# Order of the gathered tiles' work in an expert-lookup layer: dot products of both tiles ahead of the sums of both

## The chip, the cores and the metric

The kernel runs on one core of a Trainium2 chip. The metric is the device time of one execution in microseconds (us). A program of this kind keeps five engines and sixteen DMA engines busy side by side: TensorE (PE in the profile, with its weight loads as PEld), VectorE (DVE), ScalarE (ACT), GpSimd (POOL, which issues the indirect gathers here) and SyncE (SP, which issues the plain loads).

## The reference

Two transformer blocks run one after the other over 512 tokens of width 1024. The change touches only the last layer of the second block. For each token that layer picks 8 x 16 = 128 of 16,384 experts, takes the dot product of the token with each picked row of `peer_u`, applies gelu and a gate, and adds up the picked rows of `peer_v` with these factors:

```python
def chunk(args):
    hc, ec, gc = args
    u = peer_u[ec]
    a = jax.nn.gelu(jnp.einsum("ckd,cd->ck", u, hc).astype(jnp.float32)) * gc
    vv = peer_v[ec]
    return jnp.einsum("ck,ckd->cd", a.astype(vv.dtype), vv)
```

The result is added to the residual and normalised once more.

## The kernel before, in words

The 512 tokens are four tiles of 128. The kernel treats them in two ways at once, inside `peer`:

- **Dense tiles (2 and 3).** All 16,384 experts are computed. `u_tile(n)` (L1721) loads 512 KB of `peer_uT` by SP and makes 128 experts x 256 tokens on TensorE (L1726), with the gelu on ScalarE (L1728). `gates` (L1731) builds 0/1 masks on VectorE (L1759, L1760, L1764), multiplies them on TensorE (L1748, a *product*) and scales the stored activations on VectorE (L1752, *big*). `v_tile(n)` (L1772) loads 512 KB of `peer_v` and adds its four matmuls (L1776) into four accumulators.
- **Gathered tiles (0 and 1).** Only the picked rows are fetched. `row` (L1795) is one indirect DMA on the POOL queue: 128 rows of 4 KB, 512 KB, into one of 12 shared buffers (`rtile`, L1792). `dots` (L1801) fetches one row set of `peer_u` per slot and lets VectorE take its dot product (L1804), 128 slots for a tile. `factors` (L1808) makes the factors of a tile. `v_sum` (L1818) takes four row sets of `peer_v` and adds them up with eight TensorE matmuls (L1825), 32 sums for a tile. `last_norm` (L1832) finishes a tile.

The dense work is a fixed list `seq` of 256 tiles: 94 u tiles, then v and u tiles in turn until the 128th u tile, then the other v tiles. After each tile `fill` (L1864) takes gathered work from the generator `gather_units` (L1843), 1.4 row sets for each of the first 50 tiles and 2.3 after each later one. So the generator's order is the order in which gathered work enters all engines' queues, and each queue is worked off in its order. In the kernel before, the generator yields all dots of tile 0, then one sum of tile 0 and four dots of tile 1 in turn, then the sums of tile 1:

```python
yield from dots(0, 0, 128)
factors(0)
...
        if t == 0:
            yield from dots(1, 4 * r, 4 * r + 4)
```

The gate work is made in three batches of 32 steps: beside u tiles 50 to 93 (16 experts wide), beside the first 16 pairs of v and u tiles (64 wide), and beside v tiles 34 to 79 (48 wide). A row buffer is given out in turn: a gather waits until the work on the row set that lay there twelve gathers earlier is over, which is a dot on VectorE or a sum on TensorE.

Of the kernel before, what the change touches and what calls it, by code (L numbers as in the profile page):

```python
# [31 lines left out]
class Kern:  # L32
# [1430 lines left out]
    def peer(self):  # L1463
# [3 lines left out]
        GT, DT, DW = (0, 1), (2, 3), 256  # L1467
# [4 lines left out]
        with ExitStack() as ctx:  # L1472
# [5 lines left out]
            def pu(shape=(128, 512)):  # L1478
                return pp.tile(list(shape), F32, tag="u", name=self.nm("pu"), bufs=2)
# [4 lines left out]
            def pr(shape=(128, 512)):  # L1484
                return pp.tile(list(shape), F32, tag="r", name=self.nm("pr"), bufs=2)
# [309 lines left out]
            def row(src, idx):  # L1795
                u = rtile("u")
                nc.gpsimd.indirect_dma_start(out=u[:], out_offset=None, in_=A[src],  # L1797
                                             in_offset=bass.IndirectOffsetOnAxis(ap=idx, axis=0))
                return u

            def dots(t, s0, s1):  # L1801
                for s in range(s0, s1):
                    u = row("peer_u_2", ei[t][:, s:s + 1])
                    nc.vector.tensor_tensor_reduce(u[:], u[:], h3[t][:], scale=1.0, scalar=0.0, op0=OP.mult, op1=OP.add,  # L1804
                                                   accum_out=ga_t[t][:, s:s + 1])
                    yield 1

            def factors(t):  # L1808
                act(ga_t[t][:], ga_t[t][:], AF.Gelu_apprx_tanh)
                tt(ga_t[t][:], ga_t[t][:], gg[t][:], op=OP.mult)  # L1810
                p = pu([128, 4, 128])
                nc.tensor.transpose(p[:, 0, :], ga_t[t][:], self.ident[:])
                act(aT[t][:].rearrange("p g r -> p (g r)"), p[:, 0, :], AF.Copy)

            def v_rows(t, r):
                return [row("peer_v_2", eT[t][:, 32 * g + r:32 * g + r + 1]) for g in range(4)]

            def v_sum(t, r, us, acc):  # L1818

                w = wz[r % 4]  # L1820
                act(w[:, :, 31], aT[t][:, :, r], AF.Copy)  # L1821
                with ExitStack() as order:

                    for i, (c, g) in enumerate(itertools.product(range(2), (3, 0, 1, 2))):
                        m = nc.tensor.matmul(acc[c][32 * g:32 * g + 32, :], w[:, g, 31 - r:63 - r],  # L1825
                                             us[g][:, c * 512:c * 512 + 512], start=r == 0, stop=r == 31, skip_group_check=True)
                        if i == 0:
                            order.enter_context(tc.issue_after(m.ins))
# [3 lines left out]
            def last_norm(t, acc):  # L1832
                gf, x, o = rtile("gf"), rtile("xe"), rtile("xo")
                nc.gpsimd.dma_start(gf[:], rows(A["normf_g_2"], D))
                nc.gpsimd.dma_start(x[:], self.x3d[t * 128:t * 128 + 128, :])
                for c, cs in enumerate(hv):
                    tt(x[:, cs], x[:, cs], acc[c][:], op=OP.add)
                r = self.rstd([x[:, cs] for cs in hv], [o[:, cs] for cs in hv])
                for cs in hv:
                    stt(o[:, cs], x[:, cs], r[:], gf[:, cs], op0=OP.mult, op1=OP.mult)  # L1840
                    nc.sync.dma_start(self.out[t * 128:t * 128 + 128, cs], o[:, cs])

            def gather_units():  # L1843

                yield from dots(0, 0, 128)
                factors(0)
                for t in GT:
                    acc = [pr(), pr()]
                    us = v_rows(t, 0)
                    yield 4  # L1850
                    for r in range(32):
                        nx = v_rows(t, r + 1) if r < 31 else None
                        v_sum(t, r, us, acc)
                        yield 4 if r < 31 else 0
                        us = nx
                        if t == 0:
                            yield from dots(1, 4 * r, 4 * r + 4)
                    if t == 0:
                        factors(1)
                    last_norm(t, acc)  # L1860

            units = gather_units()

            def fill(n):  # L1864
# [141 lines left out]
```

## Time and profile before

| what | value |
|---|---|
| runs shown | 2919.39, 2919.87, 2923.93 us (median 2919.87) |
| the profiled execution's own time | 2930.82 us |
| its span | 2929.1 us |
| mean granted TensorE clock | 0.972 |
| PE busy in the span | 2717.2 us (93%) |
| DVE busy | 1848.5 us (63%) |
| POOL busy | 723.5 us (25%) |
| moved by DMA | 752.10 MB, mean 257 GB/s |

The layer in question begins at about 1742 us of the span, with the first u tile. The busy share of an engine over the whole span says little here. What counts is, stretch by stretch of this layer, which engine is never kept waiting, and what ends the waits of the others.

### The profile page before, as it was taken

What the parts mean: (1) busy time and instruction counts of PE and PEld (TensorE: products, weight loads), DVE (VectorE), ACT (ScalarE), POOL (GpSimd) and SP (SyncE); (2) the same over time, 40 slices, a digit from 0 to 9 for tenths busy, and PEclk for the clock granted to TensorE, in tenths of its full rate; (3) what the DMA queues carried; (4) which work ended last, traced back from release to release, by engine and by line L of the source; (5) the groups of instructions that cost most, each with busy time, mean ns of one, the idle gap of its engine ahead of it and who ended that gap; (6) DMA issues with size and microseconds to landing.
All of it is one profiled execution on the core that took longest, in us unless ns stands there. A gap on an engine that the chain in (4) does not pass through costs nothing.

```text
span 2929.1 us, 38343 instructions
## 1 busy us (share of the span) xinstructions
PE 2717.2 (93%) x13730; PEld 1907.3 (65%) x13730; DVE 1848.5 (63%) x3907; ACT 1019.7 (35%) x1672; POOL 723.5 (25%) x679
## 2 busy tenths in 40 slices
PE   7999969999999879999999889989989898699998
PEld 4776757777777667766678778877745554244333
DVE  5562569998888858998535399968557522452001
ACT  5442348777777653445633332200100000000000
POOL 1000050000000110101000343566543444444440
PEclk9999979999999989999999999999999999899999
DMA  7226568989999842322222348899988899999995
GB/s 258 87 86 215 206 212 324 355 319 354 351 351 348 317 148 86 108 72 66 89 91 94 119 166 284 335 409 409 360 326 318 327 362 350 324 355 360 369 375 184
DMA packets 228689, 752.10 MB, mean 257 GB/s; under 512 B 28160, under 2 KB 28448, under 8 KB 228496
## 3 DMA queue, kind: packets, MB, share of 16 engines
q1 hardware_dynamic: 145936, 458.69, 43.7%
q0 software_dynamic: 81984, 289.89, 27.1%
q8 instruction: 109, 1.79, 0.3%
q10 hardware_dynamic: 576, 1.05, 0.1%
q14 instruction: 84, 0.69, 0.1%
HBM read 736.90 MB, written 16.81 MB: 257 GB/s over the span
## 4 chain that ended last, share of the span: by engine, by line
PE 40%; DVE 9%; DMA 7%; issue 6%; POOL 2%; ACT 1%; DVEq 0%; another core or an unknown queue 0%; POOLq 0%; SPq 0%; ACTq 0%
PE pw L1776 12%; DMA u<-in_peer_u_dram,ei 6%; PE pu L1726 4%; PE pm L136 4%; PE pm L138 4%; PE pm L137 4%; PE pr L1825 3%; POOL u L1797 2%; DVE u L1804 2%; PE pa L1305 2%; DVE cv L1236 1%; PE pu L1748 1%; PE po L1334 1%; PE pw L138 1%; PE pw L136 1%
## 5 line engine op out<-in xcount | busy, mean ns | idle before, releaser
L84 DVE TENSOR_TENSOR lo<-raw,hi 128x1024 fp32r<-128x1024 f32 (+1 forms) x580 | 624.4, 1107 | 234.3 <-ACT hi L83 214.0
L83 ACT ACTIVATE hi<-raw 128x1024 fp32r<-128x1024 f32 (+1 forms) x600 | 556.9, 952 | 445.1 <-PE pm L137 197.0
L1804 DVE CUSTOM_DVE_ANT_0 u<-u,h 128x1024 f32<-128x1024 f32 x256 | 311.3, 1226 | 305.3 <-DMA u<-in_peer_u_dram,ei 258.7
L1726 PE MATMUL pu<-hd,raw 128*128 128x256 f32 x2048 | 474.1, 390 | 17.4 <-issue 8.3
L1776 PE MATMUL pw<-raw,big 128*128 128x512 f32 x1024 | 471.4, 609 | 6.7 <-DVE big L1752 6.7
L1726 PEld LDWEIGHTS pu<-hd,raw 128*128 128x128 f32 x2048 | 394.3, 195 | 94.9 <-issue 30.2
L1776 PEld LDWEIGHTS pw<-raw,big 128*128 128x128 f32 x1024 | 191.2, 193 | 252.7 <-issue 244.0
L1797 POOL DMA_INDIRECT u<-in_peer_v_dram,eT x256 | 259.2, 1012 | 378.5 <-DVE ga L1804 210.1
L1797 POOL DMA_INDIRECT u<-in_peer_u_dram,ei x256 | 288.4, 1126 | 204.7 <-issue 54.3
L1728 ACT ACTIVATE big<-pu 128x256 f32<-128x256 f32 x128 | 48.9, 384 | 492.6 <-PE pu L1726 430.8
L137 PE MATMUL pm<-lo,xth 128*128 128x512 f32 x512 | 204.8, 400 | 6.5 <-DVE lo L84 6.5
L136 PE MATMUL pm<-hi,xth 128*128 128x512 f32 x512 | 202.1, 395 | 0.0
L138 PE MATMUL pm<-hi,xtl 128*128 128x512 f32 x512 | 201.3, 393 | 0.0
L1236 DVE SCALAR_TENSOR_TENSOR cv<-z,cols,cv 128x496 f32<-128x496 f32 (+27 forms) x240 | 167.2, 735 | 0.5
L905 POOL DMA_INDIRECT yd<-y,idx x16 | 27.6, 1726 | 540.1 <-DVE y L1009 536.6
L138 PE MATMUL pm<-hT,lo 128*128 128x512 f32 x384 | 151.2, 395 | 0.0
L136 PE MATMUL pm<-hT,hi 128*128 128x512 f32 x384 | 151.1, 394 | 0.0
L137 PE MATMUL pm<-hT,hi 128*128 128x512 f32 x384 | 151.0, 393 | 0.0
L1821 ACT ACTIVATE wz<-aT 128x4 f32<-128x4 f32 x64 | 12.8, 209 | 396.9 <-PE pr L1825 396.8
L1825 PE MATMUL pr<-u,wz 128*32 128x512 f32 x1024 | 126.4, 612 | 8.3 <-DMA u<-in_peer_v_dram,eT 8.3
L137 PEld LDWEIGHTS pm<-lo,xth 128*128 128x128 f32 x512 | 96.4, 188 | 40.3 <-DVE lo L84 19.7
L1748 PEld LDWEIGHTS <-o 128*128 128x128 f16 x1536 | 55.0, 98 | 87.5 <-DVE big L1752 43.2
(575 smaller groups left out, 4323.8 us busy)
## 6 DMA issues: line engine op xcount, KB each, us to landing
raw<-in_w_gate_dram SPq DMA_DIRECT2D x128, 512.0 KB
raw<-in_w_up_dram SPq DMA_DIRECT2D x128, 512.0 KB
raw<-in_w_down_dram SPq DMA_DIRECT2D x128, 512.0 KB
raw<-in_peer_uT_dram SPq DMA_DIRECT2D x128, 512.0 KB
raw<-in_peer_v_dram SPq DMA_DIRECT2D x128, 512.0 KB
raw<-in_w_in_dram SPq DMA_DIRECT2D x104, 256.0 KB
wa<-in_w_ada_dram SPq DMA_DIRECT2D x48, 512.0 KB
raw<-in_w_in_dram SPq DMA_DIRECT2D x28, 512.0 KB
```

The lines of the kernel that those rows point to most:

```text
L83: return (self.nc.scalar.activation(hi, src, AF.Copy), (eng or self.nc.vector).tensor_tensor(lo, src, hi.bitcast(F32), op=OP.subtract))
L84: (eng or self.nc.vector).tensor_tensor(lo, src, hi.bitcast(F32), op=OP.subtract))
L136: mm(ps, a[0], b[0], start=first, stop=False, **kw)
L137: mm(ps, a[0], b[1], start=False, stop=False, **kw)
L138: return mm(ps, a[1], b[0], start=False, stop=last, **kw)
L1236: stt(a[:, d:], z[:, :512 - d], self.col("conv_w", k * 31 + j), a[:, d:], op0=OP.mult, op1=OP.add)
L1726: self.u_last = nc.tensor.matmul(p[:, :DW], raw[:, k, :], hd[k // 4][:, k % 4, :], start=k == 0, stop=k == KD - 1)
L1748: nc.tensor.matmul(p[:, i, :], o2[:, i // 2, :, i % 2], og[j][:, i // 2, :, i % 2], start=j == 0, stop=j == 1)
L1776: self.pace = nc.tensor.matmul(acc[t][c][:], a[:, t * 128:t * 128 + 128], raw[:, c * 512:c * 512 + 512], start=n == 0, stop=n == 127)
L1797: nc.gpsimd.indirect_dma_start(out=u[:], out_offset=None, in_=A[src], in_offset=bass.IndirectOffsetOnAxis(ap=idx, axis=0))
L1804: nc.vector.tensor_tensor_reduce(u[:], u[:], h3[t][:], scale=1.0, scalar=0.0, op0=OP.mult, op1=OP.add, accum_out=ga_t[t][:, s:s + 1])
L1825: m = nc.tensor.matmul(acc[c][32 * g:32 * g + 32, :], w[:, g, 31 - r:63 - r], us[g][:, c * 512:c * 512 + 512], start=r == 0, stop=r == 31, ...
```

## The change

The generator first yields all dots of tile 0 and tile 1, each followed by its factors, and then the sums of tile 0 and tile 1. Nothing is added or left out; the pace of `fill` stays as it is.

```diff
 def gather_units():
 
-    yield from dots(0, 0, 128)
-    factors(0)
+    for t in GT:
+        yield from dots(t, 0, 128)
+        factors(t)
     for t in GT:
         acc = [pr(), pr()]
         us = v_rows(t, 0)
...
             v_sum(t, r, us, acc)
             yield 4 if r < 31 else 0
             us = nx
-            if t == 0:
-                yield from dots(1, 4 * r, 4 * r + 4)
-        if t == 0:
-            factors(1)
         last_norm(t, acc)
```

What this does to the queues shows at two places. The first is the POOL queue in the middle of the former alternation, some fifty gathers after the last one of tile 0's dots (`in_peer_u_dram` is a row set for a dot, `in_peer_v_dram` one for a sum). Before:

```order
L1797 DMA u_18950<-in_peer_u_dram,ei_14586 128x1024
L1797 DMA u_18953<-in_peer_v_dram,eT_14587 128x1024
L1797 DMA u_18955<-in_peer_v_dram,eT_14587 128x1024
L1797 DMA u_18957<-in_peer_v_dram,eT_14587 128x1024
L1797 DMA u_18959<-in_peer_v_dram,eT_14587 128x1024
L1797 DMA u_19042<-in_peer_u_dram,ei_14586 128x1024
L1797 DMA u_19078<-in_peer_u_dram,ei_14586 128x1024
```

The same place of the queue in the changed kernel:

```order
L1797 DMA u_18922<-in_peer_u_dram,ei_14586 128x1024
L1797 DMA u_18925<-in_peer_u_dram,ei_14586 128x1024
L1797 DMA u_18961<-in_peer_u_dram,ei_14586 128x1024
L1797 DMA u_18964<-in_peer_u_dram,ei_14586 128x1024
L1797 DMA u_19006<-in_peer_u_dram,ei_14586 128x1024
```

The row sets for sums have moved behind the last dot of tile 1; four and four in turn have become one kind only.

The second is VectorE's queue in the second gate batch (`eq`, `o`, `og` are the masks, `big` the scaled activations, `ISA u_...,ga` a dot). Before:

```order
L1804 ISA u_19624,ga_15834<-u_19624,h_14592 128x1024
L1804 ISA ga_15834 128x1
L1752 SCALAR_TENSOR_TENSOR big<-pu_19394,big 128x34x8
L1752 SCALAR_TENSOR_TENSOR big_17146<-pu_19394,big_17146 128x30x8
L1759 TENSOR_TENSOR o_4214_19452<-io,e2b 128x1024
L1764 TENSOR_TENSOR og_19456<-eq_19453,gp_14595 128x512
L1764 TENSOR_TENSOR og_19458<-eq_19453,gp_14596 128x512
L1760 TENSOR_TENSOR eq_19509<-io,e1b 128x512
L1764 TENSOR_TENSOR og_19512<-eq_19509,gp_14595 128x512
L1752 SCALAR_TENSOR_TENSOR big<-pu_19433,big 128x34x8
```

The same gate batch in the changed kernel:

```order
L1804 ISA u_19465,ga_15834<-u_19465,h_14592 128x1024
L1804 ISA ga_15834 128x1
L1764 TENSOR_TENSOR og_19374<-eq_19371,gp_14595 128x512
L1764 TENSOR_TENSOR og_19376<-eq_19371,gp_14596 128x512
L1804 ISA u_19528,ga_15834<-u_19528,h_14592 128x1024
L1804 ISA ga_15834 128x1
L1752 SCALAR_TENSOR_TENSOR big<-pu_19351,big 128x34x8
L1752 SCALAR_TENSOR_TENSOR big_17146<-pu_19351,big_17146 128x30x8
L1759 TENSOR_TENSOR o_4212_19409<-io,e2b 128x1024
L1760 TENSOR_TENSOR eq_19410<-io,e1b 128x512
L1804 ISA u_19531,ga_15834<-u_19531,h_14592 128x1024
```

More dots stand between the gate steps of this batch, and none is left for the third batch. On TensorE, the first sum stood behind u tile 76; it now stands behind u tile 112 and v tile 19, where the 17th sum stood. From the 33rd sum on (behind v tile 60) both orders are the same.

## Rows read from the trace of the kernel before

**Rows 1.** Stretches of the layer (windows); columns stand in the fence's first line.

```profile
core 0: us, PE busy (x) PEld busy (x) DVE busy (x) ACT busy (x) POOL busy (x), PEclk, DMA share, GB/s
1742.00:1927.00 185.00, 175.03 (x791) 151.78 (x790) 171.20 (x715) 42.10 (x77) 85.14 (x67) 0.97 0.84 310
1927.00:2050.00 123.00, 108.17 (x721) 92.70 (x720) 96.38 (x217) 11.25 (x33) 84.75 (x65) 0.93 1.03 409
...
2050.00:2338.00 288.00, 258.96 (x1731) 172.01 (x1729) 171.59 (x397) 17.60 (x53) 127.82 (x126) 0.96 0.91 332
2338.00:2618.00 280.00, 245.47 (x1119) 124.93 (x1121) 113.29 (x235) 12.31 (x39) 129.96 (x129) 0.93 0.94 349
2618.00:2875.00 257.00, 257.00 (x1169) 99.68 (x1162) 28.03 (x79) 6.00 (x29) 112.46 (x123) 1.00 0.97 365
```

**Rows 2.** TensorE's order of time ahead of the 17th sum: start us, us, line, what.

```profile
2322.51 3.62 PE L1726 MATMUL pu<-hd,raw 128*128 128x256 f32 x16
2326.06 1.92 PE L1825 MATMUL pr<-u,wz 128*32 128x512 f32 x16
2327.91 3.70 PE L1776 MATMUL pw<-raw,big 128*128 128x512 f32 x8
2331.45 3.62 PE L1726 MATMUL pu<-hd,raw 128*128 128x256 f32 x16
```

**Rows 3.** VectorE's waits in 2050:2338: total us, times, longest us.

```profile
DVE u L1804 <- DMA u<-in_peer_u_dram,ei: 99.1, 23, 9.1
```

**Rows 4.** GpSimd's waits in 2050:2338.

```profile
POOL u L1797 <- DVE ga L1804: 111.4, 48, 5.9
POOL u L1797 <- PE pr L1825: 25.2, 10, 4.8
```

**Rows 5.** GpSimd's order of time, one round of the alternation.

```profile
2230.58 0.94 POOL L1797 DMA_INDIRECT u<-in_peer_v_dram,eT  x1 [3.74 <-DVE ga L1804]
2234.37 0.94 POOL L1797 DMA_INDIRECT u<-in_peer_u_dram,ei  x1 [2.85 <-PE pr L1825]
```

**Rows 6.** VectorE's waits in 2338:2618.

```profile
DVE u L1804 <- DMA u<-in_peer_u_dram,ei: 125.2, 13, 12.4
```

**Rows 7.** TensorE's waits in 2338:2618.

```profile
PE pu L1748 <- DVE big L1752: 26.2, 3, 17.2
PE pr L1825 <- DMA u<-in_peer_v_dram,eT: 8.3, 2, 4.6
```

**Rows 8.** VectorE's order of time ahead of TensorE's longest wait there.

```profile
2510.46 1.23 DVE L1804 CUSTOM_DVE_ANT_0 u<-u,h 128x1024 f32<-128x1024 f32 x1 [8.85 <-DMA u<-in_peer_u_dram,ei]
...
2514.90 0.61 DVE L1752 SCALAR_TENSOR_TENSOR big<-pu,big 128x112 f32<-128x112 f32 x2
```

**Rows 9.** TensorE's order of time at that wait.

```profile
2515.57 0.82 PE L1748 MATMUL pu<-og,o 128*128 128x48 f16 x16 [17.22 <-DVE big L1752]
2516.22 5.63 PE L1776 MATMUL pw<-raw,big 128*128 128x512 f32 x8
2521.68 0.56 PE L1748 MATMUL pu<-og,o 128*128 128x48 f16 x16
2522.09 1.11 PE L1776 MATMUL pw<-raw,big 128*128 128x512 f32 x2
```

**Rows 10.** TensorE's waits in 2050:2338.

```profile
PE pu L1748 <- DVE big L1752: 11.7, 5, 5.3
...
PE pw L1776 <- DVE big L1752: 6.7, 1, 6.7
```

**Rows 11.** Instructions by line in 2050:2338: busy us, mean ns, idle before, releasers.

```profile
L1804 DVE CUSTOM_DVE_ANT_0 u<-u,h 128x1024 f32<-128x1024 f32 x63 | 77.2, 1227 | 112.1 <-DMA u<-in_peer_u_dram,ei 99.1 <-issue 4.9 <-PE pu L1748 3.8
L1825 PE MATMUL pr<-u,wz 128*32 128x512 f32 x256 | 30.8, 598 | 0.0
```

**Rows 12.** The dots by line in 2338:2618.

```profile
L1804 DVE CUSTOM_DVE_ANT_0 u<-u,h 128x1024 f32<-128x1024 f32 x63 | 77.1, 1225 | 155.9 <-DMA u<-in_peer_u_dram,ei 125.2 <-issue 16.3 <-PE pr L1825 10.9
```

## The prediction

> **What bounds the kernel now.** I read the table of stretches first, cut where TensorE's order of work changes: at the first sum (2050 us), the 17th (2338), the 33rd (2618) and the end of the last one (2875). In the third stretch, 2618 to 2875, TensorE is busy for all 257 us at full clock [rows 1]: sums, v tiles and the last products run there without a wait, so that stretch lasts as long as its matmuls do. The two stretches ahead of it do not: TensorE is busy 258.96 of 288 us and 245.47 of 280, at a granted clock of 0.96 and 0.93 [rows 1]. These two, 568 us together, are where dots and sums alternate, and the only ones in which the change reorders TensorE's work.
>
> Next I asked who waits there. TensorE waits for *big* of VectorE, 26.2 us in the second stretch with 17.2 in one piece [rows 7], and 11.7 and 6.7 us in the first [rows 10]. VectorE is not overloaded, being busy 171.59 of 288 us and 113.29 of 280 [rows 1]; it waits itself, 99.1 and 125.2 us, for row sets of dots [rows 3, 6]. One place shows the chain: a dot waited 8.85 us for its rows, *big* stood behind it in VectorE's queue, and TensorE's next product came after 17.22 us of idleness [rows 8, 9]. Why the rows are late is in GpSimd's waits. A gather needs a free buffer, and the ring of 12 is mixed: gathers for sums wait for dots, and gathers for dots wait for sums, 111.4 us and 25.2 us in the first stretch [rows 4], as one round shows [rows 5]. So a row set for a dot is fetched only when TensorE has come to a sum, four arrive together, VectorE stands still until then, and the gate steps behind them are late for TensorE. Three engines wait in a ring; none is full.
>
> **The change, part by part.** *Nothing moves before 2050 us*: the orders agree up to the first sum, but for row sets fetched ahead. *Nothing moves after 2618 us* either, so what the two stretches gain or lose passes to the end one for one, since TensorE is never idle behind them. Of the 32 sums of tile 0, 16 leave the first stretch for the second; of the 126 dots of tile 1, 63 leave the second for the first [rows 11, 12].
>
> *First stretch, TensorE.* It loses 16 sums, 30.8 us [rows 11], leaving 258.96 - 30.8 = 228 us of busy time.
>
> *First stretch, VectorE.* Dots are 77.2 of its 171.59 us, so gate work is 94. With all 126 dots, at 1.227 us each [rows 11], it has 155 + 94 = 249 us. VectorE is the longest here, and 249 us is the floor. How near it gets depends on whether it still waits for rows. The row nearest to it is 1742 to 1927, dots alone beside selection work: VectorE busy 171.20 of 185 us, 0.925 [rows 1], and at that share the stretch takes 249 / 0.925 = 269 us. The other end is 1927 to 2050, dots alone beside gates: 96.38 of 123, 0.78 [rows 1], which gives 318 us. There DMA ran at 409 GB/s, a share of 1.03 [rows 1], so the rows themselves could not come faster. The first stretch moves 332 GB/s x 288 us = 95.6 MB, and in 269 us that is 355 GB/s, well under 409. So I take 0.925: 269 us, a gain of 19.
>
> *The waits that go.* With dots alone in the ring a gather waits only for the dot twelve places ahead, on the engine that needs it. The 25.2 us behind sums [rows 4] go. The 111.4 us behind dots stay in kind, but a GpSimd that waits for a busy VectorE costs nothing: VectorE then has rows in store. The gathers themselves are no bound: 127.82 us of POOL work in 288 us [rows 1], and their number in this stretch hardly changes.
>
> *The wait that is new.* `factors(1)` now stands in the middle of the tile list. Its gelu on ScalarE waits for the last dot, and u tiles' gelus stand behind it; its transpose holds TensorE, and behind that come the sums. Before, it stood where no u tile was left. This costs nothing beyond VectorE's 269 us if the dots end with the stretch, because the stretch is counted to the end of the dots.
>
> *Second stretch, TensorE.* The 16 added sums at 1.85 us (next start less start [rows 2]) are 30 us, and with the busy time it has now, at a clock of 0.93, that is 245.5 + 30 = 275 us. At full clock the work is 15 u tiles x 3.55, 41 v tiles x 3.54, 18 products x 0.41 and 32 sums x 1.85 (next start less start [rows 2, 9]), 53 + 145 + 7 + 59 = 264 us. The waits for *big* [rows 7] go with the dots: VectorE keeps 113 - 77 = 36 us of work here [rows 1, 12]. What remains is work like the third stretch's, which has no waits. I take 270, about half way, since the first sum must wait for rows queued behind the last dots: a gain of 10.
>
> *DMA.* The second stretch moves 349 GB/s x 280 us = 97.7 MB, which in 270 us is 362 GB/s; the third stretch holds 365 without a wait of TensorE [rows 1]. So it hides, barely.
>
> In this trace the 16 DMA engines carried 409 GB/s for 123 us [rows 1]. The Trainium skill, "SBUF — State Buffer", section "Summary: rules for kernel authors", reckons with about 358 GB/s between HBM and SBUF. By that rule, an estimate, the two stretches would need 267 + 273 = 540 us and could gain no more than 28. The trace disagrees with the rule in the row just named, so it sets no bound here.
>
> **Sum.** 568 - 269 - 270 = 29 us less. The profiled execution took 2930.82 us, which would become 2901.8. It stands 11 us above the median of the runs shown, 2919.87; from that I predict 2919.87 - 29 = 2891.
>
> **The rivals.**
>
> *VectorE becomes the bound (slower).* Doubling the dots in the gate batch that is heaviest for VectorE could turn its waits into TensorE's. If dots still wait for rows as in 1927 to 2050, the first stretch takes 318 us, 30 more; the second stretch keeps its gain of 10; the result is 20 slower, 2940. It decides from the point where VectorE is idle over 49 us in the first stretch (249 + 49 = 298, which eats the other gain). For it: VectorE idles 116 us there now, and the nearest stretch with dots and gates together is the poor one. Against it: that one was held by DMA at its highest rate, and TensorE's 228 us leave more room for gates. Chance 0.17.
>
> *The waits only move (no change).* If the transfers hold the rates of today, 332 and 349 GB/s, the same bytes take the same 568 us and the result is 2920. For it: the DMA share is already 0.91 and 0.94 [rows 1]. Against it: the same queues carried 409 and 365 GB/s elsewhere in this layer, so today's rates are set by who asks, not by the engines. Chance 0.13.
>
> *The change does not do what it says.* The printed order shows that it does, with dots alone and then sums alone, so I give this nothing of its own.
>
> **How the numbers follow.** The forecast has 0.70. Within it both stretches at their floors would be 249 + 264 = 513, a gain of 55, which sets the low end at 2865. The high end takes in the case of no change with the spread of the runs shown, up to 2923.93, so 2924. Left out are the slower rival and a little at the bottom, under 0.2 together. About 0.2%, 6 us, is what a measurement of this kernel can tell from no change. The forecast lies beyond that, the second rival inside it, the first beyond it on the other side: faster 0.70, same 0.13, slower 0.17.
>
> **What would show it.** In the profile after: gathers of `peer_u` in one run up to the 17th sum's old place, and no wait of GpSimd for a sum ahead of it; VectorE's waits for row sets in the first stretch down from 99 us to some 20; 126 dots there; a second stretch in which TensorE waits for *big* no more and is busy nearly throughout at full clock; a third stretch of 257 us as before. The forecast is wrong if VectorE's waits in the first stretch stay above 49 us, if TensorE stands before `factors(1)` or the first sum for more than a few us after the last dot, or if sums wait for rows in the second stretch.

## The result, and the profile after

The changed kernel takes 2880.65 us (2879.55 to 2880.92, 4 runs) against 2921.77 us before (2919.39 to 2923.93, 4 runs). The ratio is 0.9859, with a 95% interval of 0.9842 to 0.9876: 41 us less, where 29 were forecast. The time lies inside the range of 2865 to 2924.

The first view is the table of stretches of the changed kernel, cut where the stretches of before were cut: sum 0 of the changed order stands where the 17th sum stood. Columns are those of [rows 1].

```profile
core 0: us, PE busy (x) PEld busy (x) DVE busy (x) ACT busy (x) POOL busy (x), PEclk, DMA share, GB/s
...
1928.00:2051.00 123.00, 108.15 (x723) 92.62 (x722) 103.75 (x230) 11.25 (x33) 89.83 (x68) 0.93 1.03 409
2051.00:2297.00 246.00, 226.08 (x1457) 162.08 (x1455) 229.97 (x505) 14.15 (x37) 150.55 (x118) 0.97 0.98 372
2297.00:2569.00 272.00, 271.87 (x1391) 131.04 (x1395) 40.99 (x115) 16.07 (x55) 124.76 (x133) 1.00 0.98 368
2569.00:2825.00 256.00, 256.00 (x1167) 99.20 (x1159) 26.51 (x75) 5.89 (x29) 113.50 (x123) 1.00 0.98 373
```

Against [rows 1] the first stretch fell from 288 to 246 us and the second from 280 to 272; the third is 256 instead of 257. In the second stretch TensorE is now busy for 271.87 of 272 us at full clock. In the first VectorE is busy for 229.97 of 246 us, a share of 0.935.

The next view is the waits of VectorE, then of GpSimd, in the first stretch of the changed kernel (total us, times, longest us).

```profile
DVE u L1804 <- DMA u<-in_peer_u_dram,ei: 13.5, 21, 1.3
DVE big L1752 <- PE pu L1748: 2.6, 1, 2.6
```

```profile
POOL u L1797 <- DVE ga L1804: 57.3, 34, 4.5
POOL u L1797 <- issue: 21.3, 54, 4.7
POOL u L1797 <- DMA u<-in_peer_u_dram,ei: 8.4, 13, 1.2
```

VectorE's waits for row sets, 99.1 us in 23 pieces before [rows 3], are 13.5 us in 21, none over 1.3 us. GpSimd waits for no sum any more, where it waited 25.2 us [rows 4]. TensorE's four longest waits of the first stretch and its only one of the second:

```profile
PE pw L1776 <- DMA raw<-in_peer_v_dram: 5.3, 3, 3.8
PE pw L1748 <- DVE o L1759: 4.6, 1, 4.6
PE pu L1726 <- issue: 3.6, 3, 2.4
PE pw L1776 <- DVE big L1752: 2.5, 1, 2.5
```

```profile
PE pr L1825 <- DMA u<-in_peer_v_dram,eT: 0.7, 1, 0.7
```

The 26.2 us behind *big* in the second stretch [rows 7] are gone.

Two profiles of one kernel need not agree, so the kernel before was profiled once more.

**Run b_again**, no edit.

> The kernel before, unchanged, profiled a second time. Both theories expect the same: 2920 us (2917 to 2925). It tells whether the profiled execution of before, 2930.8 us and so 11 us above its other runs, was an odd one, and so how many of the 50 us between the two profiles are the change's and how many that execution's.

It took 2923.62 us with a span of 2921.9, where the first profile had 2929.1:

```profile
2048.00:2332.00 284.00, 258.82 (x1716) 170.52 (x1720) 171.48 (x397) 17.20 (x53) 126.00 (x127) 0.96 0.93 336
2332.00:2611.00 279.00, 244.29 (x1117) 124.28 (x1121) 113.80 (x237) 12.30 (x39) 128.27 (x128) 0.94 0.95 351
2611.00:2867.00 256.00, 256.00 (x1164) 99.50 (x1160) 26.63 (x78) 5.88 (x28) 113.32 (x123) 1.00 0.98 366
```

So 7 of the 50 us between the first two profiles were that execution's. Against this profile the change gains 284 - 246 = 38 us in the first stretch and 279 - 272 = 7 in the second; the first stretch begins 3 us later in the changed kernel, 2051 instead of 2048. 38 + 7 - 3 = 42, which is the difference of the spans within a microsecond (2921.9 - 2879.2 = 42.7). Of the 45 us that the two stretches lose, 40 are idle time of TensorE: it was busy for 503.1 of 563 us and is busy for 498.0 of 518. The other 5 go with a higher granted clock (0.96 and 0.94 before, 0.97 and 1.00 after).

### The profile page after: what moved, and what is told of

It is laid out like the page before. It is cut to its first block, busy times and chain, and to the rows that moved or that the text cites. A ratio compares the mean times of both kernels' runs of the same rounds, so it can differ in the third digit from the quotient of the medians.

```text
span 2879.2 us, 38219 instructions
## 1 busy us (share of the span) xinstructions
PE 2711.3 (94%) x13730; PEld 1904.1 (66%) x13730; DVE 1841.6 (64%) x3907; ACT 1020.6 (35%) x1672; POOL 746.7 (26%) x679
## 4 chain that ended last, share of the span: by engine, by line
PE 39%; DVE 10%; DMA 8%; issue 5%; POOL 2%; ACT 1%; DVEq 0%; POOLq 0%; ACTq 0%; SPq 0%
PE pw L1776 13%; DMA u<-in_peer_u_dram,ei 7%; PE pr L1825 4%; PE pm L136 4%; PE pm L138 4%; PE pm L137 4%; PE pu L1726 2%; DVE u L1804 2%; POOL u L1797 2%; PE pa L1305 2%; DVE cv L1236 1%; PE po L1334 1%; PE pw L138 1%; PE pw L136 1%; PE pw L137 1%
## 5 line engine op out<-in xcount | busy, mean ns | idle before, releaser
L1797 POOL DMA_INDIRECT u<-in_peer_u_dram,ei x256 | 323.2, 1263 | 239.8 <-DVE ga L1804 89.1
L1797 POOL DMA_INDIRECT u<-in_peer_v_dram,eT x256 | 247.2, 966 | 269.2 <-PE pr L1825 199.7
L1764 DVE TENSOR_TENSOR og<-eq,gp 128x128 f16<-128x128 f16 (+2 forms) x192 | 58.9, 332 | 276.8 <-PE pu L1748 273.0
L1728 ACT ACTIVATE big<-pu 128x256 f32<-128x256 f32 x128 | 48.9, 384 | 503.4 <-PE pu L1726 503.1
```

Of the source, the lines that this page charges most:

```text
L1764: tt(o[:], eq[:], by2(gp[j], t0, w), op=OP.mult)
```

## Experiments

Two theories were tried first. **A**: the cost was the alternation of dots and sums in one queue and one ring of buffers. **B**: the cost was the place of the dots, beside the third gate batch, which the change has cleared.

**Run sums_first: no alternation, but dots beside the third batch.**

```diff
                         us = nx
-                        if t == 0:
-                            yield from dots(1, 4 * r, 4 * r + 4)
-                    if t == 0:
-                        factors(1)
                     last_norm(t, acc)
+                    if t == 0:
+                        yield from dots(1, 0, 128)
+                        factors(1)
```

> Order: dots of tile 0, sums of tile 0, dots of tile 1, sums of tile 1. Nothing alternates, but the dots of tile 1 fall beside the third gate batch. Theory A (the alternation of row sets in one ring and one queue is what costs): the gain stays, 2880 to 2895 us, and VectorE's waits for row sets fall below 60 us in the two stretches. Theory B (what counts is that no dots stand beside the third gate batch): with 126 dots x 1.22 us = 154 us of VectorE ahead of its masks TensorE waits for it, by over 40 us, and the time is 2920 us or more.

It took 2884.03 us (2882.09 to 2885.14), ratio 0.9868 (0.9849 to 0.9887): nearly all of the gain. Its two stretches:

```profile
2051.00:2335.00 284.00, 284.00 (x1992) 177.44 (x1989) 109.29 (x279) 24.25 (x72) 123.00 (x130) 1.00 0.93 337
2335.00:2563.00 228.00, 203.73 (x812) 113.06 (x811) 173.43 (x330) 5.79 (x15) 160.11 (x123) 0.95 1.03 409
```

TensorE's waits for VectorE and VectorE's for row sets, in the second of them:

```profile
PE pu L1748 <- DVE big L1752: 18.0, 2, 17.2
PE pu L1748 <- DVE og L1764: 5.8, 3, 4.3
```

```profile
DVE u L1804 <- DMA u<-in_peer_u_dram,ei: 54.3, 69, 1.4
```

With sums alone TensorE is never kept waiting for 284 us, though it has 16 sums more there than before. With dots alone DMA runs at 409 GB/s and VectorE waits 54.3 us, in pieces of at most 1.4 us where they were up to 12.4 [rows 6]. Theory B expected over 40 us of TensorE's waits beside the third batch; there are 24. Both ways of ending the alternation gain about the same, so its end is what the change's gain has in common with this run's. The 3 us between them lie within the intervals of the two ratios, so these two runs show no worth of the dots' place.

**Run eight: the alternation kept, the third batch mostly cleared.** Eight dots after each of the first 16 sums.

```diff
-                        if t == 0:
-                            yield from dots(1, 4 * r, 4 * r + 4)
-                    if t == 0:
-                        factors(1)
+                        if t == 0 and r < 16:
+                            yield from dots(1, 8 * r, 8 * r + 8)
+                            if r == 15:
+                                factors(1)
```

> The alternation stays, but with eight dots after each sum instead of four, so that the dots of tile 1 are through after 16 sums and most of them stand ahead of the third gate batch. Theory A (alternation costs): VectorE still waits for row sets about as long per burst as before, and only the waits of TensorE in the third batch, 26 us, can go: 2895 to 2910 us. Theory B (placement costs): most of the gain is had, 2880 to 2890 us.

It took 2921.88 us, ratio 0.9998 (0.9983 to 1.0012): nothing gained, less than either theory expected. VectorE still waits for row sets in its first stretch, which now holds more dots and lasts 302 us instead of 284; the second lasts 258 instead of 279:

```profile
DVE u L1804 <- DMA u<-in_peer_u_dram,ei: 94.5, 39, 8.7
```

```profile
2049.00:2351.00 302.00, 262.07 (x1665) 178.15 (x1662) 200.87 (x451) 16.77 (x49) 144.33 (x134) 0.93 0.92 329
2351.00:2609.00 258.00, 243.05 (x1178) 122.57 (x1177) 83.83 (x182) 13.10 (x44) 120.95 (x122) 0.97 0.97 357
```

TensorE no longer waits for *big* beside the third batch, but has a new wait of 15 us. Its waits in the second stretch, then ScalarE's order of time there:

```profile
PE pu L1726 <- ACT big L1728: 15.0, 1, 15.0
```

```profile
2427.82 0.39 ACT L1728 ACTIVATE big<-pu 128x256 f32<-128x256 f32 x1 [6.50 <-PE pu L1726]
2461.37 0.31 ACT L1809 ACTIVATE ga<-ga 128x128 f32<-128x128 f32 x1 [33.16 <-DVE ga L1804]
2461.58 0.36 ACT L1728 ACTIVATE big<-pu 128x256 f32<-128x256 f32 x1
```

This is the new wait that the prediction named: the gelu of `factors(1)` stands at the head of ScalarE's queue until the last dot is done, and the u tiles' gelus behind it. In the changed kernel ScalarE waits 4.9 us there and TensorE does not.

**Run eight_late: the same, `factors(1)` put back behind the sums.**

```diff
-                            if r == 15:
-                                factors(1)
+                    if t == 0:
+                        factors(1)
                     last_norm(t, acc)
```

> The run with eight dots per sum, but with the factors of tile 1 made behind the sums of tile 0, where no u tile is left, instead of right behind its last dot. In the former run ScalarE waited 33 us for the last dot with the gelu of those factors at the head of its queue, and TensorE 15 us behind it. If that wait hid what the new place of the dots gains: 2900 to 2910 us. If it is covered by other waits: 2918 to 2925 us, and clearing the third gate batch of dots is worth nothing while the alternation stays.

It took 2920.33 us, ratio 0.9996 (0.9984 to 1.0009). The run does not answer its question: the scheduler set the gelu, which needs nothing but the dots, where it had been, and only its transpose moved. TensorE's wait is still there, 14.1 us:

```profile
PE pu L1726 <- ACT big L1728: 14.1, 1, 14.1
```

Whether clearing the third batch alone would gain up to those 15 us stays open. If the other waits stay as they are, it can't be more, and the change gains 41.

**Run split: two rings.** While dots and sums alternate, dots have 4 of the 12 buffers and sums 8; elsewhere both rings are used in turn.

```diff
+            turn = itertools.count()
-            def rtile(nm):
-                return gr.tile([128, D], F32, tag="u", name=self.nm(nm), bufs=12)
+            def rtile(nm, tag=None):
+                tag = tag or ("u" if next(turn) % 3 == 0 else "v")
+                return gr.tile([128, D], F32, tag=tag, name=self.nm(nm), bufs=4 if tag == "u" else 8)
...
-                    u = row("peer_u_2", ei[t][:, s:s + 1])
+                    u = row("peer_u_2", ei[t][:, s:s + 1], "u" if t else None)
...
-                return [row("peer_v_2", eT[t][:, 32 * g + r:32 * g + r + 1]) for g in range(4)]
+                return [row("peer_v_2", eT[t][:, 32 * g + r:32 * g + r + 1], None if t else "v") for g in range(4)]
```

> The order of before, but the 12 row buffers are two rings while dots and sums alternate: 4 for dots, 8 for sums. A gather for a dot then no longer waits for a sum's buffer. If the shared ring is the cause of the waits: GpSimd's waits for sums ahead of dots' gathers go, VectorE's waits for row sets in the two stretches fall from 224 us to 110 or less, and the time is 2890 to 2905 us. If the one POOL queue is the cause, in which dots' gathers stand behind those for sums whatever their buffers: waits stay above 180 us and the time is 2915 to 2925 us.

It took 2914.76 us, ratio 0.9971 (0.9958 to 0.9984). GpSimd's waits for sums in the first stretch all but go (1.3 us, from 20.3 in the second profile of before). VectorE's waits for row sets over both stretches fall from 213.9 us in that profile to

```profile
DVE u L1807 <- DMA u<-in_peer_u_dram,ei: 158.0, 64, 9.7
```

The time lies just below the second expectation's range, the waits lie between the two. But the edit moved more than the rings. With buffers of their own the dots ran ahead, and 94 of them lie in the first stretch, where there were 63 [rows 11]:

```profile
L1807 DVE CUSTOM_DVE_ANT_0 u<-u,h 128x1024 f32<-128x1024 f32 x94 | 114.5, 1224 | 90.8 <-DMA u<-in_peer_u_dram,ei 90.6
```

As in the run with eight dots per sum, that stretch grew (304 us) and the second shrank (248). TensorE no longer waits for *big* in the second, but its sums wait 13.9 us for rows there. So separate rings gain some 8 us as they were built here, and how much of that is the ring itself is not shown. What keeps the dots waiting with rings of their own is not settled either: one queue for both kinds remains, but a ring of four holds only four rows in store. These were not tried apart.

**Run one_by_one: a finer alternation.** One row set for the next sum and one dot in turn, in place of four and four.

```diff
+                        if t == 0:
+                            nx, g = [], dots(1, 4 * r, 4 * r + 4)
+                            for i in range(4):
+                                if r < 31:
+                                    nx.append(row("peer_v_2", eT[t][:, 32 * i + r + 1:32 * i + r + 2]))
+                                    yield 1
+                                yield next(g)
+                            next(g, None)
+                            v_sum(t, r, us, acc)
...
-                        if t == 0:
-                            yield from dots(1, 4 * r, 4 * r + 4)
```

> The order of before, but inside the alternation the row sets are fetched in turn one by one (one for the next sum, one dot, and so on) instead of four and four; ring, count and place in the tile list stay. If the bunching of four is what makes VectorE wait: its waits for row sets are much shorter, in sum under 120 us in the two stretches, and the time is 2890 to 2905 us. If it is the coupling of dots to sums through the ring: 2912 to 2925 us.

It took 2959.72 us, ratio 1.0130 (1.0107 to 1.0154): slower by 38 us, which neither reading expected. VectorE's waits, then TensorE's, in its second stretch (2350 to 2647 us):

```profile
DVE u L1804 <- DMA u<-in_peer_u_dram,ei: 81.6, 29, 6.1
DVE u L1804 <- issue: 76.8, 23, 5.5
```

```profile
PE pu L1748 <- DVE big L1752: 28.7, 4, 15.9
PE pr L1825 <- DMA u<-in_peer_v_dram,eT: 22.9, 5, 7.6
```

The single waits are shorter than before (6.1 us at most, from 12.4 [rows 6]) but VectorE still waits at least as long in sum, and TensorE's sums now wait longer for rows, 22.9 us where it was 8.3 [rows 7]. So taking turns more finely did not help. It does not show that bunching costs nothing, because the edit changes something else too: each sum now stands behind the round's four dots, where it stood ahead of them. By the generator's order the first row set of a sum is followed by 15 gathers before the sum frees it, where 11 followed before, and the ring holds 12. The finer turns and the fuller ring were not tried apart.

**Run after8: the changed order with 8 buffers.**

```diff
-                return gr.tile([128, D], F32, tag="u", name=self.nm(nm), bufs=12)
+                return gr.tile([128, D], F32, tag="u", name=self.nm(nm), bufs=8)
```

> The changed order with 8 row buffers instead of 12. If the change gains because dots have twelve row sets in store rather than some four, a third less store costs: 2890 to 2905 us, with VectorE's waits for row sets in the first stretch above 30 us (13.5 in the changed kernel). If it gains because nothing alternates, little is lost: 2880 to 2886 us.

It took 2905.39 us, ratio 0.9939 (0.9921 to 0.9957), 25 us above the changed kernel. The time is about that of the first expectation, the place is not: VectorE's waits for rows in the first stretch are 17.1 us, not over 30, and the stretch lengthens by 6 us only. Some 13 us are lost ahead of the first stretch, where the changed kernel and the one before are nearly alike (195 and 126 us here, 185 and 123 there). So the number of buffers counts outside the change's stretches too, and it can't be all that the change gave: with 8 buffers and no alternation the kernel is still 16 us ahead of 12 with it. The kernel before was not run with 8.

**Runs p215, p205_24 and p195_25: the pace.** In the first stretch of the changed kernel TensorE is busy for 226 of 246 us while VectorE and DMA are nearly full; later TensorE is the bound. Fewer row sets per tile early, more later:

```diff
-                room = fill(room + (1.4 if acc is None and n < NA else 2.3))
+                room = fill(room + (1.4 if acc is None and n < NA else 2.05 if j < 126 else 2.4))
```

The other two have 2.15 throughout, and 1.95 and 2.5.

> The changed order at a slower pace, 2.15 row sets per tile instead of 2.3, so that the gathered work ends at tile 255 of 256 instead of 242. If VectorE and DMA are the bound of the first stretch of the changed kernel (TensorE busy 226 of 246 us), fewer dots per tile there give 5 to 12 us: 2869 to 2876 us. If the last sums come too late for the end, it is 2880 to 2890 us.

> The changed order with 2.05 row sets per tile up to tile 126 of the list, 2.4 from there. If the first stretch of the changed kernel is bound by VectorE and DMA while the later ones have room in DMA: 2868 to 2875 us. If the later stretches' DMA has no room left (they carry 368 to 373 GB/s), sums wait for rows there and the gain is lost: 2880 us.

2879.31 us (2870.27 to 2883.37) for 2.15, which is no difference and lies just short of the slower of its two expectations; 2874.04 us (2866.03 to 2875.1) for 2.05 and 2.4. Ratios 0.9860 (0.9841 to 0.9879) and 0.9838 (0.9822 to 0.9855). The second was run again beside the changed kernel, with a further step.

> The changed kernel, unchanged, beside the two below on the same chip: 2880 us (2876 to 2885).

> The changed order with 2.05 row sets per tile up to tile 126 and 2.4 after it, once more, beside the changed kernel: if the 7 us between them in earlier runs is the pace, 0.997 to 0.998 of it, about 2873 us; if it was the spread of runs, the same 2880 us.

> A further step the same way, 1.95 and 2.5. If VectorE and DMA still hold the first stretch (TensorE waits 12 of 265 us there at 2.05): 2866 to 2872 us. If DMA of the later stretches is now the bound (2.5 row sets and one plain tile per tile of work are 3.5 x 524,288 B, 390 GB/s at 4.7 us): sums wait for rows and the time is 2875 us or more.

On one chip the changed kernel took 2879.79 us (2878.01 to 2882.04), the slower early pace 2868.90 (2863.35 to 2872.68) and the further step 2868.88 (2865.42 to 2872.74); ratios to before 0.9858 (0.9843 to 0.9873), 0.9817 (0.9802 to 0.9832) and 0.9818 (0.9804 to 0.9831). So the pace is worth another 11 us here, 7 in the earlier runs and by the expectation, and the version with 2.05 and 2.4 beats both kernels. In its profile TensorE is busy without a wait from the first sum on, at 2316 us:

```profile
2051.00:2316.00 265.00, 252.21 (x1567) 181.93 (x1563) 228.89 (x501) 16.96 (x48) 151.09 (x121) 0.98 0.98 376
2316.00:2575.00 259.00, 259.00 (x1383) 119.30 (x1386) 48.49 (x136) 13.85 (x49) 120.46 (x129) 1.00 0.97 362
2575.00:2822.00 247.00, 247.00 (x1086) 94.37 (x1078) 17.74 (x51) 5.88 (x28) 113.08 (x123) 1.00 1.00 382
```

The dots' stretch, which now holds more tiles, lasts 265 us with 13 of TensorE idle, where it was 246 with 20. The later ones stay full. The further step finds nothing more to take: TensorE idles 14 us in its first stretch, and the third is at 390 GB/s with a first wait of a sum for rows, 1.0 us:

```profile
2579.00:2816.00 237.00, 235.98 (x1060) 89.15 (x1052) 16.69 (x48) 5.88 (x28) 113.39 (x123) 1.00 1.00 390
```

## Why the prediction was right, point by point

- **The ring of waits.** Right, and shown from two sides: both kernels without the alternation gain about 40 us, and the one that keeps it but moves the dots gains nothing. Which part of it costs most, the ring of buffers or the one queue, is not settled: the runs with two rings and with finer turns each changed more than one thing.
- **Nothing moves outside the two stretches.** The third stretch is 256 us, after 257 and 256 in the two profiles of before. Ahead of the first not quite: eight or nine more dots ran there, since buffers that had held row sets for sums now hold row sets for dots (11 gathers from 1927 to 2050 fetched rows for sums before, none does now). VectorE is busy 103.75 us from 1928 to 2051 against 96.38 [rows 1].
- **The first stretch, predicted at 269, measured 246.** This is the term of the sum that was mis-sized. VectorE's work there was put at 249 us and called a floor. It is 229.97. About half of the difference is that 117 dots are left there instead of 126, the others having run ahead. The other half is the price of a dot: the 1.227 us are the length of its record, but when rows are in store the next instruction starts before the record ends. Back to back, as below, a dot takes 1.15 us, so that 126 of them are 145 us and not 155. The gate work has hardly changed (*o*, the largest part, is 48 instructions of 679 ns; before, 48 of 686). The share of 0.925, taken from the nearer of two rows, came out at 0.935.

```profile
L1804 DVE CUSTOM_DVE_ANT_0 u<-u,h 128x1024 f32<-128x1024 f32 x117 | 140.8, 1219 | 13.9 <-DMA u<-in_peer_u_dram,ei 13.5
```

```profile
2281.20 1.22 DVE L1804 CUSTOM_DVE_ANT_0 u<-u,h 128x1024 f32<-128x1024 f32 x1
...
2282.35 1.22 DVE L1804 CUSTOM_DVE_ANT_0 u<-u,h 128x1024 f32<-128x1024 f32 x1
```

- **The second stretch, predicted at 270, measured 272.** Right with its reason: no wait for *big*, full clock. One u tile of about 3.5 us, which stood ahead of the cut before, now runs behind it (256 matmuls of u tiles in this stretch, 240 before). Counted on the same work, the first stretch gained some 35 us against the second profile of before, and the second some 10.
- **DMA.** Predicted to hide at 355 and 362 GB/s; it ran at 372 and 368, a share of 0.98, so it hides, with little to spare. The Trainium skill, "SBUF — State Buffer", section "Summary: rules for kernel authors", reckons with about 358 GB/s between HBM and SBUF, by which, in the prediction's estimate, no more than 28 us could have been gained. The measured rates and the gain of 41 us are above that, so here the measurement decides.
- **`factors(1)`.** Named as a wait that would cost nothing if the dots end with the stretch. In the changed kernel that holds. The run with eight dots per sum shows its price where they don't: 15 us.
- **The slower rival** needed VectorE idle for over 49 us in the first stretch; it was idle for 246 - 230 = 16.
- **The baseline.** The first stretch of the profile shown, 288 us, is 284 in the second one. The forecast of 29 us was worked out from an execution some 7 us longer than that one; from the 563 us of the second profile the same two stretches give 24. That the time lies in the stated range says little by itself, as the range takes in no change at all; what speaks for the account is the waits that went.

## What to carry to other kernels

Where two consumers on different engines share one in-order queue of transfers, or one ring of buffers, each holds the other's rows back: look for an engine that waits though nothing is full, and ask who must free the buffer that its next transfer needs. Give one consumer the queue for a while and then the other, rather than taking turns; the one run with finer turns, in which the ring was fuller too, was slower. When a step that feeds on the last item of such a run is moved, see what stands behind it in its engine's queue, and set the pace stretch by stretch, by what is full there.

## What was not expected of the hardware

A gather takes longer on GpSimd when it begins while VectorE is in a dot. This is from the first stretch of the changed kernel, both engines in order of time:

```profile
2227.74 1.22 DVE L1804 CUSTOM_DVE_ANT_0 u<-u,h 128x1024 f32<-128x1024 f32 x1
2228.08 1.68 POOL L1797 DMA_INDIRECT u<-in_peer_u_dram,ei  x1 [2.27 <-DVE ga L1804]
...
2229.49 0.74 DVE L1752 SCALAR_TENSOR_TENSOR big<-pu,big 128x272 f32<-128x272 f32 x2
2230.06 0.94 POOL L1797 DMA_INDIRECT u<-in_peer_u_dram,ei  x1 [0.30 <-issue]
```

The first gather began 0.34 us into a dot, took 1.68 us and ended 0.80 us after the dot did. The second began beside *big* and took 0.94. Over the whole of that trace, 233 gathers began while VectorE was idle, and none of them took over 0.99 us; 166 began in a dot, and 135 of these took over 1.00, up to 1.99.

It is not the load of the DMA engines. At 390 GB/s, in the third stretch of the run with 1.95 and 2.5, where VectorE is busy for 16.69 of 237 us, a gather took 0.94 us. At 310 GB/s, from 1742 to 1927 of the kernel before, where VectorE is busy for 171.20 of 185 us [rows 1], it took 1.29:

```profile
L1797 POOL DMA_INDIRECT u<-in_peer_v_dram,eT x117 | 110.2, 941 | 110.5 <-PE pr L1825 73.7 <-issue 17.4 <-PE pw L1776 8.7
```

```profile
L1797 POOL DMA_INDIRECT u<-in_peer_u_dram,ei x67 | 86.1, 1285 | 105.4 <-DVE ga L1804 28.1 <-DVE mr L1536 19.1 <-DVE mr L1563 15.2
```

So 118 gathers in the dots' stretch of the changed kernel keep GpSimd busy for 150.55 us, where 126 took 127.82 before [rows 1]. It was still no bound there, as it waited 57.3 us for dots. Why a dot holds a gather back is not shown by these runs.

The 16 DMA engines carried 409 GB/s for the 228 us of the second stretch of the run with sums first, gathers and plain loads together.
